# Gate and up of a channel mixer by seven products of quarters, with the matmuls pinned in the program's order

## The chip, the cores and the metric

The kernel runs on one core of one Trainium2 chip. The metric is the device time of one execution in microseconds (us). PE is the matrix engine (TensorE), PEld its weight loads, DVE VectorE, ACT ScalarE, POOL GpSimd, SP the engine that issues the DMAs of the weights.

## What is computed

A trunk of two layers on x of 256 tokens by 1024, all in float32. Each layer has a channel mixer, an attention part and a second channel mixer:

```python
for l in range(DEPTH):                      # 2
    x = x + 0.5 * swiglu(rms_norm(x, n1[l]), w_gate1[l], w_up1[l], w_down1[l])
    h = rms_norm(x, mix_norm[l])
    qa, ka, va, qb, kb, vb = split(h @ w_in[l])      # 1024 x 2304
    out_a = windowed_gqa_sink(qa, ka, va, sink[l])   # 8 heads, 2 key heads, ALiBi
    out_b = rms_norm(differential_attention(qb, kb, vb, lam)) * (1 - lam_init)   # 4 heads
    x = x + concat(out_a, out_b) @ w_out[l]          # 1024 x 1024
    x = x + 0.5 * swiglu(rms_norm(x, n2[l]), w_gate2[l], w_up2[l], w_down2[l])
return rms_norm(x, final_norm)
# swiglu(h, g, u, d) = (silu(h @ g) * (h @ u)) @ d, with g and u 1024 x 2816, d 2816 x 1024
```

The four mixers hold most of the arithmetic.

## The kernel before

**Products.** Every float32 factor is split in two parts of the type fp32r: `hi`, a rounded copy, and `lo`, what is left over. A product is three matmuls, hi times hi, lo times hi and hi times lo, added up in PSUM. For a product by tokens (`tokens`, lines 323 to 325) the activations are the stationary operand, 128 x 128, and 512 columns of weights stream past. `narrow` (lines 344 to 346) does it the other way round for the attention projections, with 256 tokens streaming.

**Weights.** A list `specs` holds all weight tiles in the order of use; most are 4 chunks of 128 rows by 512 columns (1 MB). `weights()` hands out the next tile and emits the loads up to two places ahead (`LOOK`). `emit_load` issues the DMA into `raw` (line 93), then for each half of the tile a cast on ACT (`whi`, line 109) and a subtraction on DVE (`wlo`, line 110). There are three buffers each of raw, whi and wlo. A scheduler orders each engine's instructions ahead of time by a simulated timeline; work inside `urgent()` has priority.

**A mixer** (`ffn`) works on the 2816 hidden columns in five groups of 512 and one of 256 (`NGRP` = 5). Group g computes gate and up (two tiles each, rows 0 to 511 and 512 to 1023, for both halves of the tokens: 96 matmuls), then the hidden by Silu on ACT (`gate`, line 395) and a scalar_tensor_tensor on DVE (`up`, line 401). Its down projection (two tiles, 48 matmuls) is done after the gate and up of group g + 1, from the hidden turned by transposes on PE (`turn`, line 415) and split in hi and lo (`split`, lines 329 and 330). Group 0 has no down of its own; its first two tiles, gate and up, are used in turns. After the last whole group come the quarter groups' gate and up in one tile, the down of group 4 for the left half of the output, the down of the remainder (`end`), and the down of group 4 for the right half. The down products stay in four of the eight PSUM banks throughout.

**Between stages.** `ffn_close` adds each finished half to the residual `xk` (line 375), transposes it (`Norm.pair`, line 182) and makes the next norm's operands: a scaled copy on ACT (line 190) and the left-over on DVE (line 191). The right half is turned inside the next stage (`late`).

**Attention** (`mix`) computes projections, scores, softmax, the two heads' outputs (`osl`, line 628; `oa`, line 670), the norm of the differential heads (`norm_b`, Squares at line 645), transposes them (`turned`, line 635) and multiplies by w_out.

Of the kernel before, what the change touches and what calls it, by code (L numbers as in the profile page):

```python
# [14 lines left out]
P = 128  # L15
# [7 lines left out]
HB = 4  # L23
# [4 lines left out]
LOOK = 2  # L28
N_RAW, N_HI, N_LO = 3, 3, 3
N_S4 = 18  # L30
# [3 lines left out]
def trunk(ctx: ExitStack, tc: tile.TileContext, x, n1, g1, u1, d1, nm, w_in, sink,  # L34
# [29 lines left out]

    def urgent():

        return tc.high_priority(300)


    specs = []  # L70
    loaded = {}
# [7 lines left out]
    def plain(w, c0, n, k0=0, kn=None):  # L79
        src = rows(w, c0, n, k0, kn)  # L80
        kn = src.shape[1]
        return (kn, n, lambda t: [(t, src)])

    def emit_load(i):
        kn, n, moves = specs[i]
        raw = wp.tile([P, kn, n], F32, tag="raw", bufs=N_RAW, name=nm_("raw"))
# [4 lines left out]
        for dst, src in moves(raw):  # L91
            if i > 1:
                sp.dma_start(dst, src)
            else:
                for a, b in zip(cuts, cuts[1:]):
                    sp.dma_start(dst[:, a:b], src[:, a:b])
                    yield
# [15 lines left out]
    nxt = [0, 0]  # L113

    def weights():
        i = nxt[0]
        nxt[0] += 1
        while i > 1 and nxt[1] <= min(i + LOOK, len(specs) - 1):
            for _ in emit_load(nxt[1]):
                pass  # L120
            nxt[1] += 1
        return loaded.pop(i)

    for l in range(DEPTH):
        def ffn_specs(wg, wu, wd):
# [3 lines left out]
            for g in range(1, NGRP):  # L129
                specs.extend(plain(w[l], g * 512, 512, k0, 4) for w in (wg, wu) for k0 in (0, 4))  # L130
                specs.extend(down(g - 1, h) for h in range(2))
            for k0 in (0, 4):
                def gu_moves(t, k0=k0, ws=(wg[l], wu[l])):
                    return [(t[:, :, h * 256:h * 256 + 256], rows(w, FF - 256, 256, k0, 4)) for h, w in enumerate(ws)]
                specs.append((4, 512, gu_moves))
# [10 lines left out]
        for c in range(2):  # L146
# [3 lines left out]
            specs.append((KC, 256, qa_moves))  # L150
# [5 lines left out]
        for k0 in (0, 2):  # L156
# [3 lines left out]
            specs.append((2, D, o_moves))  # L160
# [6 lines left out]
    class Norm:  # L167


        def __init__(self, g0):  # L170
            self.g0, self.xs = g0, []
            self.ss = tmp("nss", 2, (P, 2, 4))

        def squares(self, t, c, n):
            j_ = tmp("junk", 2, (P, 512))
            act.activation(j_[:, :n], xk[:, t, c:c + n], AF.Square, accum_out=self.ss[:, t, c // 256:c // 256 + 1])

        def pair(self, j):
            sl = halves(bank())
            for i in range(2):  # L180
                for t in range(2):
                    pe.transpose(sl[:, i, t * P:(t + 1) * P], xk[:, t, (2 * j + i) * P:(2 * j + i + 1) * P], ident)  # L182
            with urgent():
                self.operands(j, sl)

        def operands(self, j, sl):
            xs = blk()
            for i in range(2):
# [4 lines left out]
            self.xs.append(xs)  # L193
# [11 lines left out]
        def spread(self, sl):  # L205
# [4 lines left out]
            pe.matmul(sl[:, 0:S], lhsT=ones, rhs=dg, start=True, stop=True)  # L210
# [8 lines left out]
    early = [emit_load(0), emit_load(1)]  # L219
# [4 lines left out]
    nxt[1] = 2  # L224
# [27 lines left out]
    dist_i = const.tile([P, 512], mybir.dt.int32, name="dist_i")  # L252
# [7 lines left out]
    lin = const.tile([P, 4, DEPTH * 64], F32, name="lin")  # L260
    lsum = const.tile([P, 2, DEPTH], F32, name="lsum")
    lpr = const.tile([P, 2, DEPTH * 64], F32, name="lpr")
# [6 lines left out]
    def attention_constants():  # L269
# [6 lines left out]

        pool.iota(dist_i, pattern=[[P, 2], [-1, S]], base=0, channel_multiplier=1)
# [21 lines left out]

        for i, a in enumerate((lq1, lk1, lq2, lk2)):  # L300
            pool.dma_start(lin[:, i], a.rearrange("l d -> (l d)").partition_broadcast(P))

    def make_lam():
        for i in range(2):
# [11 lines left out]
    def tokens(accs, xs, w, k0, ks=range(4), first=0, last=KC - 1, tc=None):  # L316

        hi, lo = w
        for k, t in (tc or [(k, t) for k in ks for t in range(2)]):
# [3 lines left out]
            pe.matmul(accs[t], lhsT=xh, rhs=hi[:, k], start=kk == first, stop=False)  # L323
            pe.matmul(accs[t], lhsT=xl, rhs=hi[:, k], start=False, stop=False)  # L324
            pe.matmul(accs[t], lhsT=xh, rhs=lo[:, k], start=False, stop=kk == (last if isinstance(last, int) else last[t]))  # L325
# [11 lines left out]
    def narrow(acc, w, j, xs, kcs, first, last):  # L337

        hi, lo = w
        for i, (wk, xk) in enumerate(kcs):  # L340
# [3 lines left out]
            pe.matmul(acc, lhsT=wh, rhs=xv[:, 0:S], start=first and i == 0 and j == 0, stop=False)  # L344
            pe.matmul(acc, lhsT=wh, rhs=xv[:, S:512], start=False, stop=False)  # L345
            pe.matmul(acc, lhsT=wl, rhs=xv[:, 0:S], start=False, stop=last and i == len(kcs) - 1 and j == 1)  # L346
# [43 lines left out]
    def ffn(norm, aside=None, before=None, final=False):  # L390
# [11 lines left out]

        def hidden(gs, us):
# [5 lines left out]
        def turn(hs, n):  # L409
            out_ = []  # L410
            for i in range(n):
                sl = halves(bank())
                for c in range(2):
                    for t in range(2):
                        pe.transpose(sl[:, c, t * P:(t + 1) * P], hs[:, t, (2 * i + c) * P:(2 * i + c + 1) * P], ident)  # L415
# [8 lines left out]
        def down(hT, g, h, w):  # L424
            tokens(accs[h], [None] * (2 * g) + hT, w, 4 * g, last=(FC - 1, 4 * (NGRP - 1) - 1) if final and h else FC - 1)
# [42 lines left out]

        def end(h, tc=None, acc=None, c=0):
# [333 lines left out]
```

## Time and profile before

| what | us |
|---|---|
| median of three runs | 977.82 (977.58 to 980.34) |
| profiled execution | 978.65 |
| its span, from the first to the last instruction | 976.8 |
| PE busy | 954.5 |
| DVE busy | 549.9 |
| ACT busy | 475.7 |
| mean granted clock of PE | 0.996 |

Busy time says how long an engine had an instruction under way; matmuls overlap, so their own durations (390 ns) add up to more than PE's busy time, and the distance between their starts is what counts. A group line gives the busy time, the mean duration of one, then the idle time ahead of such instructions with what ended it.

### The profile page before, as it was taken

To read this page: it belongs to the slowest core of one execution; us is meant where nothing else is said; L and a number is where in the kernel's file an instruction comes from. 1 tells how busy PE (TensorE), PEld (TensorE's weight loads), DVE (VectorE), ACT (ScalarE), POOL (GpSimd) and SP (SyncE) were. 2 spreads that over 40 slices of the span, in tenths; PEclk is the share of its full clock that TensorE was granted. 3 is DMA by queue.
4 is the path that set the end of the run, shared out by engine and by line. 5 is a ranking of instruction groups with operands and counts; after the bars stand their busy time and mean duration, and the time that the engine had idled before them with its cause. 6 is when DMAs were issued, how large, how long until landed. Compare 5 with 4: busy or idle time off the path is not lost.

```text
span 976.8 us, 12379 instructions
## 1 busy us (share of the span) xinstructions
PE 954.5 (98%) x4940; PEld 809.3 (83%) x4940; DVE 549.9 (56%) x844; ACT 475.7 (49%) x809; POOL 21.2 (2%) x50
## 2 busy tenths in 40 slices
PE   7999999999999999999999999999999999999996
PEld 5888888889888888888878888887998888888885
DVE  5745445569846454555555454556696465545453
ACT  5644444457835543443544434436577464434442
POOL 3000000000000000000000000000000000000001
PEclk9999999999999999999999999999999999999999
DMA  9765555544524665555545656656444256565541
GB/s 269 260 206 182 174 193 193 176 135 166 131 85 143 211 206 175 194 191 179 193 144 181 201 181 188 197 174 196 148 140 122 87 172 205 182 211 198 173 129 43
DMA packets 98217, 169.38 MB, mean 173 GB/s; under 512 B 3182, under 2 KB 30896, under 8 KB 98160
## 3 DMA queue, kind: packets, MB, share of 16 engines
q1 hardware_dynamic: 96784, 167.26, 53.3%
q0 software_dynamic: 288, 0.30, 0.4%
q10 hardware_dynamic: 1088, 1.05, 0.3%
q8 instruction: 38, 0.62, 0.3%
q14 instruction: 19, 0.16, 0.1%
HBM read 167.54 MB, written 1.05 MB: 173 GB/s over the span
## 4 chain that ended last, share of the span: by engine, by line
PE 95%; DMA 2%; ACT 2%; issue 0%; DVE 0%; SPq 0%; POOLq 0%; POOL 0%; ACTq 0%
PE ps L323 26%; PE ps L324 26%; PE ps L325 26%; PE ps L344 3%; PE ps L345 3%; PE ps L346 3%; PE ps L415 2%; DMA raw<-in_ffn_w_gate_dram 2%; PE ps L670 1%; PE ps L523 1%; ACT whi L109 1%; PE ps L609 1%; PE ps L610 1%; PE ps L611 1%; PE ps L628 1%; PE ps L182 1%
## 5 line engine op out<-in xcount | busy, mean ns | idle before, releaser
L110 DVE TENSOR_TENSOR wlo<-raw,whi 128x1024 fp32r<-128x1024 f32 (+2 forms) x392 | 379.5, 1013 | 319.7 <-ACT whi L109 317.8
L109 ACT CAST whi<-raw 128x1024 fp32r<-128x1024 f32 (+2 forms) x392 | 323.3, 882 | 360.4 <-PE ps L324 327.7
L324 PE MATMUL ps<-whi,s 128*128 128x512 f32 x1126 | 438.3, 389 | 0.0
L323 PE MATMUL ps<-whi,s 128*128 128x512 f32 x1126 | 433.5, 392 | 3.1 <-ACT s L190 2.0
L325 PE MATMUL ps<-wlo,s 128*128 128x512 f32 x1126 | 436.4, 389 | 0.0
L323 PEld LDWEIGHTS ps<-whi,s 128*128 128x128 f32 x1126 | 211.3, 188 | 46.6 <-ACT s L190 2.2
L324 PEld LDWEIGHTS ps<-whi,s 128*128 128x128 f32 x1126 | 212.0, 188 | 43.4 <-DVE ms L197 0.4
L325 PEld LDWEIGHTS ps<-wlo,s 128*128 128x128 f32 x1126 | 211.8, 188 | 43.5
L344 PE MATMUL ps<-s,whi 128*128 128x256 f32 x224 | 63.3, 287 | 4.3 <-ACT s L190 4.3
L345 PE MATMUL ps<-s,whi 128*128 128x256 f32 x224 | 63.6, 285 | 0.0
L346 PE MATMUL ps<-s,wlo 128*128 128x256 f32 x224 | 63.1, 283 | 0.0
L395 ACT ACTIVATE tmp<-ps,r 128x512 f32<-128x512 f32 (+1 forms) x48 | 31.3, 651 | 61.3 <-PE ps L325 61.3
L401 DVE SCALAR_TENSOR_TENSOR s<-ps,hr,tmp 128x512 f32<-128x512 f32 (+1 forms) x48 | 32.6, 705 | 35.6 <-PE ps L325 26.0
L344 PEld LDWEIGHTS ps<-s,whi 128*128 128x128 f32 x224 | 42.4, 191 | 5.3 <-ACT s L190 4.8
L345 PEld LDWEIGHTS ps<-s,whi 128*128 128x128 f32 x224 | 42.9, 192 | 0.2
L346 PEld LDWEIGHTS ps<-s,wlo 128*128 128x128 f32 x224 | 42.9, 192 | 0.2
L330 DVE TENSOR_TENSOR s<-ps,s 128x512 fp32r<-128x512 f32 x48 | 30.9, 682 | 8.2 <-ACT s L329 8.2
L533 ACT ACTIVATE s<-s,negm 128x256 f32<-128x256 f32 x64 | 31.8, 499 | 7.6 <-DVE negm L531 7.6
L329 ACT CAST s<-ps 128x512 fp32r<-128x512 f32 x48 | 25.7, 583 | 12.0 <-PE ps L415 9.7
L190 ACT ACTIVATE s<-ps,gcol 128x256 fp32r<-128x256 f32 x48 | 20.7, 472 | 7.4 <-PE ps L182 4.1
L415 PE MATMUL ps<-ident,s 128*128 128x128 f32 x176 | 23.8, 272 | 0.0
L415 PEld LDWEIGHTS ps<-ident,s 128*128 128x128 f32 x176 | 20.7, 140 | 3.2
(114 smaller groups left out, 414.5 us busy)
## 6 DMA issues: line engine op xcount, KB each, us to landing
raw<-in_ffn_w_down_dram SPq DMA_DIRECT2D x44, 1024.0 KB, 5.0
raw<-in_ffn_w_gate_dram SPq DMA_DIRECT2D x39, 1024.0 KB, 5.2
raw<-in_ffn_w_up_dram SPq DMA_DIRECT2D x39, 1024.0 KB, 5.1
raw<-in_w_in_dram SPq DMA_DIRECT2D x14, 1024.0 KB, 5.3
raw<-in_ffn_w_gate_dram SPq DMA_DIRECT2D x8, 512.0 KB, 4.0
raw<-in_ffn_w_up_dram SPq DMA_DIRECT2D x8, 512.0 KB, 5.0
raw<-in_w_in_dram SPq DMA_DIRECT2D x8, 512.0 KB, 4.6
raw<-in_w_out_dram SPq DMA_DIRECT2D x4, 1024.0 KB, 4.9
```

Of the source, the lines that this page charges most:

```text
L109: act.copy(h_, r_)
L110: dve.tensor_tensor(l_, r_, f(h_), op=ALU.subtract)
L323: pe.matmul(accs[t], lhsT=xh, rhs=hi[:, k], start=kk == first, stop=False)
L324: pe.matmul(accs[t], lhsT=xl, rhs=hi[:, k], start=False, stop=False)
L325: pe.matmul(accs[t], lhsT=xh, rhs=lo[:, k], start=False, stop=kk == (last if isinstance(last, int) else last[t]))
L344: pe.matmul(acc, lhsT=wh, rhs=xv[:, 0:S], start=first and i == 0 and j == 0, stop=False)
L345: pe.matmul(acc, lhsT=wh, rhs=xv[:, S:512], start=False, stop=False)
L346: pe.matmul(acc, lhsT=wl, rhs=xv[:, 0:S], start=False, stop=last and i == len(kcs) - 1 and j == 1)
L395: act.activation(g[:, :n], acc, AF.Silu, scale=norm.r[:, t:t + 1])
L401: dve.scalar_tensor_tensor(h[:, t, :n], in0=acc, scalar=norm.hr[:, t:t + 1], in1=g, op0=ALU.mult, op1=ALU.mult)
L415: pe.transpose(sl[:, c, t * P:(t + 1) * P], hs[:, t, (2 * i + c) * P:(2 * i + c + 1) * P], ident)
L533: act.activation(e[:, t, c], e[:, t, c], AF.Exp, scale=-1.0, bias=negm[:, n:n + 1], accum_out=den[:, n:n + 1])
```

## The change

Three of the whole groups (1, 3 and 4) compute gate and up together by a scheme of seven products in place of eight (Strassen's, in Winograd's form). The activations are cut in quarters by tokens and by rows of the weights, the weights in four: a is the upper half of gate, b of up, c the lower half of up, d of gate. Four sums of activation quarters are made once per mixer (`make_sums`). The seven weight operands are, in order of use, a, b - a, c - b, c - b + a, d, d - c + b - a and c, made in place in the raw tiles by differences on DVE (`less`) before the usual cast and subtraction. Each product is 12 matmuls into one bank; `by_seven` adds them up on DVE with a copy of the first on ACT. A changed group has nine weight tiles to split in place of six, of which six are loaded.

The transposes of the hidden before come after the second product. All matmuls that go through `mm` and all transposes that go through `flip` are pinned behind the instruction of PE that is traced before them. DMA and splitting of a weight tile are emitted apart; raw has six buffers and the loads run up to eight places ahead. The end of a mixer is put in a new order (`ffn_end`), and so are Squares and one scaled copy in attention. The constants for attention are made ahead of group 3; some buffers are shared or fewer.

```diff
-LOOK = 2
-N_RAW, N_HI, N_LO = 3, 3, 3
-N_S4 = 18
+LOOK, AHEAD = 2, 8
+N_RAW, N_HI, N_LO = 6, 3, 3
+N_S4 = 16
+SEVEN = (1, 3, 4)
...
+    def mm(*a, **k):
+
+        tc.keep_in_program_order(pe.matmul(*a, **k))
+
+    def flip(*a):
+        tc.keep_in_program_order(pe.transpose(*a))
...
+    class Step:
+        def __init__(self, kn, n, moves, key=None, prep=None, src=None, free=None):
+            self.kn, self.n, self.moves, self.prep = kn, n, moves, prep
+            self.key = object() if key is None else key
+            self.src = self.key if src is None else src
+            self.free = [self.src] if free is None else free
...
+    def seven(wg, wu, c0, downs):
+
+        a, b, c, d = [object() for _ in range(4)]
+
+        def less(x, y, to):
+
+            def prep():
+                for h in (0, 2):
+                    x_, y_, t_ = [raws[i][:, h:h + 2] for i in (x, y, to)]
+                    dve.tensor_tensor(t_, x_, y_, op=ALU.subtract)
+            return prep
+
+        n = dict(kn=4, n=512, moves=None)
+        return [plain(wg, c0, 512, 0, 4, key=a, free=[]),
+                Step(4, 512, plain(wu, c0, 512, 0, 4).moves, key=b, prep=less(b, a, a), src=a, free=[]),
+                Step(4, 512, plain(wu, c0, 512, 4, 4).moves, key=c, prep=less(c, b, b), src=b),
+                Step(**n, prep=less(c, a, a), src=a, free=[]),
+                downs[0],
+                plain(wg, c0, 512, 4, 4, key=d, free=[]),
+                Step(**n, prep=less(d, a, d), src=d, free=[a, d]),
+                Step(**n, src=c),
+                downs[1]]
...
+    def emit_dma(i):
+        s = specs[i]
+        raws[s.key] = raw = wp.tile([P, s.kn, s.n], F32, tag="raw", bufs=N_RAW, name=nm_("raw"))
+        for dst, src in s.moves(raw):
+            if i > 1:
+                sp.dma_start(dst, src)
+            else:
+                for k in range(s.kn):
+                    sp.dma_start(dst[:, k:k + 1], src[:, k:k + 1])
+                    yield
+
+    def emit_split(i):
+        s = specs[i]
+        kn, n, raw = s.kn, s.n, raws[s.src]
         hi = wp.tile([P, kn, n], F32R, tag="whi", bufs=N_HI, name=nm_("whi"))
         lo = wp.tile([P, kn, n], F32R, tag="wlo", bufs=N_LO, name=nm_("wlo"))
...
+    at = dict(use=0, dma=2, prep=2, split=2)
 
     def weights():
-        i = nxt[0]
-        nxt[0] += 1
-        while i > 1 and nxt[1] <= min(i + LOOK, len(specs) - 1):
-            for _ in emit_load(nxt[1]):
-                pass
-            nxt[1] += 1
+        i = at["use"]
+        at["use"] += 1
+        if i > 1:
+            while True:
+
+                if at["split"] <= min(i + LOOK, len(specs) - 1) and at["prep"] > at["split"]:
+                    for _ in emit_split(at["split"]):
+                        pass
+                    at["split"] += 1
+                elif at["prep"] <= min(i + LOOK + 1, len(specs) - 1) and at["dma"] > at["prep"] and \
+                        (specs[at["prep"]].prep is None or at["split"] >= at["prep"]):
+                    if specs[at["prep"]].prep is not None:
+                        specs[at["prep"]].prep()
+                    at["prep"] += 1
+                elif at["dma"] < min(i + AHEAD, len(specs)) and (specs[at["dma"]].moves is None or len(raws) < N_RAW):
+                    if specs[at["dma"]].moves is not None:
+                        for _ in emit_dma(at["dma"]):
+                            pass
+                    at["dma"] += 1
+                else:
+                    break
         return loaded.pop(i)
...
+            if self.sums:
+                if j % 2 == 0:
+                    self.xg.append(blk(F32).rearrange("p a (c s) -> p (a c) s", c=2))
+                for i in range(2):
+                    act.activation(self.xg[j // 2][:, j % 2 * 2 + i], sl[:, i], AF.Identity,
+                                   scale=gcol[:, self.g0 + 2 * j + i:self.g0 + 2 * j + i + 1])
+                if j == 3:
+                    self.make_sums()
...
+        def make_sums(self):
+
+            (t0, t1), (b0, b1) = [(t[:, :, 0:P], t[:, :, P:S]) for t in self.xg]
+            self.sm = []
+
+            def make(x, y, op):
+                v = tmp().rearrange("p a (c s) -> p (a c) s", c=2)
+                dve.tensor_tensor(v, x, y, op=op)
+                sm = blk().rearrange("p a (c s) -> p (a c) s", c=2)
+                act.copy(sm[:, :, 0:P], v)
+                dve.tensor_tensor(sm[:, :, P:S], v, f(sm[:, :, 0:P]), op=ALU.subtract)
+                self.sm.append(sm)
+                return v
+
+            s1 = make(t1, b1, ALU.add)
+            s2 = make(s1, t0, ALU.subtract)
+            make(t0, t1, ALU.subtract)
+            make(b0, s2, ALU.subtract)
+
+        def quarter(self, t, b):
+
+            def of(k):
+                xv = self.xs[2 * b + k // 2][:, k % 2]
+                return xv[:, t * P:(t + 1) * P], xv[:, S + t * P:S + (t + 1) * P]
+            return of
+
+        def summed(self, i):
+            return lambda k: (self.sm[i][:, k, 0:P], self.sm[i][:, k, P:S])
...
+        def prod(xo):
+            hi, lo = weights()
+            acc = bank()
+            for k in range(4):
+                xh, xl = xo(k)
+                mm(acc, lhsT=xh, rhs=hi[:, k], start=k == 0, stop=False)
+                mm(acc, lhsT=xl, rhs=hi[:, k], start=False, stop=False)
+                mm(acc, lhsT=xh, rhs=lo[:, k], start=False, stop=k == 3)
+            return acc
+
+        def by_seven(h, g):
+
+            flat = lambda: tmp().rearrange("p a n -> p (a n)")
+
+            def plus(o, x, y):
+                with urgent():
+                    dve.tensor_tensor(o, x, y, op=ALU.add)
+                return o
+
+            acc = prod(norm.quarter(0, 0))
+            m1 = flat()
+            with urgent():
+                act.copy(m1, acc)
+            m5 = prod(norm.summed(0))
+            hT = turn(h, 2)
+            m7 = prod(norm.summed(2))
+            m6 = prod(norm.summed(1))
+            u2 = plus(flat(), m1, m6)
+            u3 = plus(flat(), u2, m7)
+            u1 = plus(flat(), u3, m5)
+            plus(u2, u2, m5)
+            down(hT, g - 1, 0, weights())
+            acc = prod(norm.quarter(0, 1))
+            h = blk(F32)
+            g0 = plus(m1, m1, acc)
+            with urgent():
+                act.activation(g0, g0, AF.Silu, scale=norm.r[:, 0:1])
+            acc = prod(norm.quarter(1, 1))
+            g1 = plus(u3, u3, acc)
+            with urgent():
+                act.activation(g1, g1, AF.Silu, scale=norm.r[:, 1:2])
+            up(h, u1, g1, 1)
+            acc = prod(norm.summed(3))
+            plus(u2, u2, acc)
+            up(h, u2, g0, 0)
+            down(hT, g - 1, 1, weights())
+            return h
+
...
         for g in range(1, NGRP):
-            if g > 1:
-                hT = turn(h, 2)
+            if g == 3 and aside is not None:
+                with tc.issue_after(norm.last.ins):
+                    aside()
+            if g in SEVEN:
+                h = by_seven(h, g)
+                continue
             gs = [bank(), bank()]
             tokens(gs, norm.xs, weights(), 0)
-            if g == 1:
-                hT = turn(h, 2)
+            hT = turn(h, 2)
             tokens(gs, norm.xs, weights(), 4)
             us = [bank(), bank()]
             for k0 in (0, 4):
@@ -453,34 +615,48 @@
             h = hidden(gs, us)
             for hh in range(2):
                 down(hT, g - 1, hh, weights())
-            if g == 2 and aside is not None:
-                with tc.issue_after(norm.last.ins):
-                    aside()
-
+
+        gu = [bank(), bank()]
+        tokens(gu, norm.xs, weights(), 0)
         hT = turn(h, 2)
-        gu = [bank(), bank()]
-        for k0 in (0, 4):
-            tokens(gu, norm.xs, weights(), k0)
+        tokens(gu, norm.xs, weights(), 4)
         h = hidden([b[:, 0:256] for b in gu], [b[:, 256:512] for b in gu])
-        down(hT, NGRP - 1, 0, weights())
-        hE = [None] * (2 * NGRP) + turn(h, 1)
-        wE = [t.rearrange("p k (h n) -> p h k n", h=2) for t in weights()]
-
-        def end(h, tc=None, acc=None, c=0):
-            tokens(accs[h] if acc is None else [acc, acc], hE, [t[:, h, :, c:c + 512 if acc is None else c + 256] for t in wE],
-                   4 * NGRP, range(2), 0, FC - 1, tc)
-
-        return accs, hT, end, weights
+        return accs, hT, lambda: turn(h, 1)
+
+    BY_TOKENS = [(k, t) for t in range(2) for k in range(2)]
+    G4 = 4 * (NGRP - 1)
+
+    def ffn_end(parts, last):
+
+        accs, hT, rest = parts
+        hT = [None] * (2 * (NGRP - 1)) + hT
+        hE = []
+        w = {0: weights()}
+
+        def group(h, order, a=None, c=slice(None), first=0):
+            tokens(a or accs[h], hT, [t[:, :, c] for t in w[h]], G4, first=first, last=last[h], order=order)
+
+        def tail(h, order=BY_TOKENS, a=None, c=slice(None)):
+            tokens(a or accs[h], [None] * (2 * NGRP) + hE, [t[:, h, :, c] for t in w["rest"]], 4 * NGRP, last=last[h], order=order)
+
+        group(0, [(k, t) for k in range(3) for t in range(2)])
+        hE.extend(rest())
+        group(0, [(3, t) for t in range(2)])
+        w["rest"] = [t.rearrange("p k (h n) -> p h k n", h=2) for t in weights()]
+        w[1] = weights()
+        return group, tail
 
     def ffn_close(parts, nxt):
-        accs, hT, end, w = parts
-        res = Residual(nxt, accs)
-        end(0, [(k, t) for t in range(2) for k in range(2)])
+        group, tail = ffn_end(parts, (FC - 1, G4 + 3))
+        res = Residual(nxt, parts[0])
+        group(1, [(0, t) for t in range(2)])
+        tail(0)
         for t in range(2):
             res.add(0, t)
-        tokens(accs[1], [None] * (2 * (NGRP - 1)) + hT, w(), 4 * (NGRP - 1), first=0, last=FC - 1)
+        tail(1)
+        group(1, [(k, t) for k in (1, 2) for t in range(2)])
         res.turn(0)
-        end(1, [(k, t) for t in range(2) for k in range(2)])
+        group(1, [(3, t) for t in range(2)])
         for t in range(2):
             res.add(1, t)
 
...
-        for t in range(2):
-            act.activation(vB[:, t], vsl[t], AF.Copy, scale=norm.r[:, t:t + 1])
+        act.activation(vB[:, 0], vsl[0], AF.Copy, scale=norm.r[:, 0:1])
+        dve.tensor_scalar_mul(vB[:, 1], vsl[1], norm.r[:, 1:2])
...
         def norm_b():
 
             ss = tmp("ss", 1, (P, 2, HB))
-            for h in range(HB):
-                for t in range(2):
-                    j_ = tmp("junk", 2, (P, P))
-                    act.activation(j_, osl[t][:, h * P:(h + 1) * P], AF.Square, accum_out=ss[:, t, h:h + 1])
+            for t in range(2):
+                sq = tmp().rearrange("p a n -> p (a n)")
+                act.activation(sq, osl[t], AF.Square)
+                dve.tensor_reduce(ss[:, t], sq.rearrange("p (h d) -> p h d", h=HB), axis=mybir.AxisListType.X, op=ALU.add)
...
-                        pe.matmul(oa[t][:, c * P + a * 64:c * P + a * 64 + 64], lhsT=pT[c][:, kc, c0:c0 + P],
+                        mm(oa[t][:, c * P + a * 64:c * P + a * 64 + 64], lhsT=pT[c][:, kc, c0:c0 + P],
...
```

Elsewhere `pe.matmul` and `pe.transpose` become `mm` and `flip` in `tokens`, `narrow`, `spread`, `pair`, `turn` and `turned`; the scores, the transposed probabilities and the value products stay as they were. Norms ahead of attention make no sums. The last mixer's end uses `ffn_end` too.

More of the change, by code (lines that the diff above doesn't have):

```diff
@@ L313, in make_lam, with tokens @@
             dve.tensor_scalar_mul(gsub[:, l:l + 1], gcol[:, 48 + l:49 + l], 1.0 - lam_init[l])
-    def tokens(accs, xs, w, k0, ks=range(4), first=0, last=KC - 1, tc=None):
+    def tokens(accs, xs, w, k0, ks=range(4), first=0, last=KC - 1, order=None):
         hi, lo = w
-        for k, t in (tc or [(k, t) for k in ks for t in range(2)]):
+        for k, t in (order or [(k, t) for k in ks for t in range(2)]):
             kk = k0 + k
@@ L753, in finish @@
             sp.dma_start(out[0, t * P:(t + 1) * P, j * 512:(j + 1) * 512], ob[:, j])
[L755 to L756 removed]
+    accs = parts[0]
+    group, tail = ffn_end(parts, ((FC - 1), FC - 1))
+    dve.tensor_tensor(xk[:, 1, 512:D], xk[:, 1, 512:D], accs[1][1], op=ALU.add)
+    group(1, [(k, 0) for k in range(2)])
+    tail(0)
     for t in range(2):
         close(t, 0, 512, accs[0][t])
[L759 to L763 removed]
+    group(1, [(k, 0) for k in (2, 3)])
+    tail(1, [(k, 0) for k in range(2)])
     close(0, 512, 512, accs[1][0])
@@ L767, in trunk @@
         acc = bank()[:, 0:256]
-        cols = [t[:, :, c:c + 256] for t in w]
-        tokens([None, acc], hT, cols, 4 * (NGRP - 1), first=4 * (NGRP - 1), last=FC - 1, tc=[(k, 1) for k in range(4)])
-        end(1, [(k, 1) for k in range(2)], acc, c)
+        cols = slice(c, c + 256)
+        group(1, [(k, 1) for k in range(4)], [None, acc], cols, G4)
+        tail(1, [(k, 1) for k in range(2)], [None, acc], cols)
         close(1, 512 + c, 256, acc)
```

96 lines of the change are left out of this document (45 added, 51 removed).

## The prediction

> **What bounds the kernel now.** I read the busy times first, then the waits of the matrix engine (PE), then one steady group of a channel mixer in three views: the windows, the costliest groups of instructions, and VectorE's (DVE's) timeline.
>
> ```profile
> PE 954.5 (98%) x4940; PEld 809.3 (83%) x4940; DVE 549.9 (56%) x844; ACT 475.7 (49%) x809; POOL 21.2 (2%) x50
> ```
>
> PE is busy 98% of 976.8 us: products that go away can pay in full, if whoever feeds PE keeps up. The waits of PE over the whole run (what waited, for whom: us in total, times, longest):
>
> ```profile
> PE ps L344 <- ACT s L190: 4.3, 2, 2.1
> PE ps L323 <- ACT s L190: 2.0, 1, 2.0
> PE ps L323 <- ACT s L658: 0.9, 2, 0.5
> PE ps L628 <- ACT v L617: 0.6, 2, 0.3
> ```
>
> Besides 6.5 us at the start, all PE waits for lies at joints of stages: three of some 2 us where a mixer ends and the next norm's operands (L190) are late, four below 0.5 us in attention. A steady group, and the clock behind the third joint (us, busy us of PE, PEld, DVE, ACT, POOL, granted clock, DMA):
>
> ```profile
> 391.40:424.90 33.50, 33.50 (x154) 27.81 (x153) 16.79 (x16) 14.10 (x17) 0.00 (x0) 1.00 0.58 188
> 491.00:494.70 3.70, 3.70 (x15) 3.22 (x14) 3.05 (x8) 2.36 (x6) 0.69 (x1) 0.54 0.85 270
> ```
>
> One group of 512 columns takes 33.5 us, PE without a gap; DVE works for half of it. DVE's part, and the forms that the change multiplies:
>
> ```profile
> L110 DVE TENSOR_TENSOR wlo<-raw,whi 128x1024 fp32r<-128x1024 f32 x256 | 302.1, 1221 | 296.2 <-ACT whi L109 294.4
> L109 ACT CAST whi<-raw 128x1024 fp32r<-128x1024 f32 x256 | 256.0, 1050 | 307.9 <-PE ps L324 306.7 <-DMA raw<-in_ffn_w_gate_dram 1.0
> L375 DVE TENSOR_TENSOR xk<-xk,ps 128x512 f32<-128x512 f32 x20 | 13.1, 682 | 4.4 <-PE ps L325 4.4
> ```
> ```profile
> 394.51 1.28 DVE L330 TENSOR_TENSOR s<-ps,s 128x512 fp32r<-128x512 f32 x2
> 409.47 2.36 DVE L110 TENSOR_TENSOR wlo<-raw,whi 128x1024 fp32r<-128x1024 f32 x2 [2.96 <-ACT whi L109]
> 413.37 1.43 DVE L401 SCALAR_TENSOR_TENSOR s<-ps,hr,tmp 128x512 f32<-128x512 f32 x2 [1.54 <-PE ps L325]
> ```
>
> Two instructions back to back start 2.36 - 1.22 = 1.14 us apart at 1024 elements, 1.28 - 0.68 = 0.60 at 512, 1.43 - 0.75 = 0.68 for L401: a queue is summed by these. ACT's cast waits for PE (306.7 us): a weight tile is split when PE has left the tile three places earlier, and DVE's idle time hangs on that. DVE's slack is what the change spends.
>
> **Matmuls.** In the timeline a tile of 24 matmuls lasts 5.44 us, 0.2265 each. Seven products of 12 take 84 instead of 96: 2.72 us less, so a changed group needs 33.5 - 2.7 = 30.8 us of PE. There are 12 (3 in each of 4 mixers): 32.6 us if PE stays the bound.
>
> **DVE in a changed group.** Before: 6 tiles at 2.28 (two halves), two ups, two splits of the turned hidden: 13.7 + 1.4 + 1.2 = 16.3 (the window has 16.8). After: 9 tiles (7 weight operands, 2 of down) 20.5; four differences of weights, two instructions each, 9.1 (no such f32 result of 1024 elements is in the trace; L110 is the same operation on the same operands in size and place, so 1.14; below it nothing speaks, above it 1.22 if none overlap); 7 additions with PSUM or tmp at 0.60 (L375's form) 4.2; ups 1.4, splits 1.2. Sum 36.4, and about 0.7 because four or five of the additions read what the instruction before them wrote (L281 to L282 in the start: 0.72 apart instead of 0.60). So 37.1 of DVE against 30.8 of PE: DVE becomes the bound of these groups unless it enters them with work done. The page "VectorE: DVE Perf Modes" of the Trainium skill (The TRN2 errata) gives (N+151)/0.96 ns for an f32 tensor_tensor, 1.224 us at 1024; L110's 1.221 agrees for one. Charged in full to each of the 26 long instructions this makes the group 2.2 us dearer and would turn the sum below to about 992 (pair 70.9, group 1 34.5); the 1.14 between starts decides against it.
>
> ACT: 9 tiles at 2 x 0.95, a copy, two Silus, two casts: about 21 of 30.8, no bound.
>
> **The lead.** Three buffers of whi and wlo: when PE starts a group's first product, DVE can have done A and B, and the differences for B and for C (they write raw, of which there are now six): 4 x 2.28 = 9.1. At the end, the last tile's second half must be ready 2.7 us before PE ends, and behind it come 1.3 (an addition, an up). One group alone, with full lead: 37.1 - 9.1 - 1.3 + 2.7 = 29.4, under 30.8, so hidden.
> - Group 3 follows a plain group, in which DVE is idle for half: 30.8.
> - Group 4 follows group 3 at once: the two need 74.2 - 9.1 - 1.3 + 2.7 = 66.5, before 67.0: -0.5 for the pair.
> - Group 1 follows group 0, whose first two tiles are held together and released late, and whose ups (1.4) and second half of B (1.1) fall into it: 29.4 + 2.5 = 31.9, with a Silu ahead of B's cast 32.3: -1.2.
> Together -1.7 per mixer, -6.8. Bounds: no lead at all, 37.1 in each, +3.6 x 12 = +43; all hidden, -32.6. I take the queue's sum because each of its rows is measured; only the lead is argued.
>
> **Sums of the activations**: 8 DVE instructions at 0.60, 4 casts at 0.54, 8 activations at 0.38 (L190) per mixer norm, in group 0, where DVE idles 4.3 us in one piece ahead of the next tiles' casts. Hidden there; if ACT is late, up to 3 us each. I take +0.3 x 4 = +1.2.
>
> **Joints.** The three waits of 2.15, 2.15, 1.97 stand behind eight transposes (L182) that were queued after the last matmul (195.62 against 195.40). Pinned in program order, they get 6 matmuls (1.36 us) and the second pair's transposes behind them as cover, against some 2 us that ACT and DVE need for the operands: I keep 0.6 each, so -4.5. The half clock behind the third (0.54 for 3.7 us in the window) goes with it: -1.7. Bounds: 0, if a cast or subtraction stands ahead in the queues; -8.0. The ffn's turned remainder gets 12 matmuls, 2.7 us, over a split of about 1.5: nothing.
>
> **Attention.** norm_b's eight Squares and their reads become two activations and two reductions, shortening the chain by over 1 us; its transposes are now ahead of the last 8 products (L670), which cover them; one vB goes to DVE. Of 1.5 us of waits I take back 1.2. If the chain of some 4.5 us outlasts the 24 products ahead (5.3 us by the 0.11 between records of L670), it costs 1 us per layer.
>
> **Start.** Split into DMA and splits with six raw buffers, the loads stay in one queue in order. The pinned order takes the scheduler's freedom to put matmuls on whi ahead of those on wlo, and the extra activations stand among the first casts: +1.0 (0 to 2.5). Fewer or renamed buffers (s4 16, junk 1) wait for nothing that is alive by my count: 0.
>
> **Sum**: -6.8 + 1.2 - 6.2 - 1.2 + 1.0 = -12.0. The profiled execution took 978.65 (span 976.8), 0.83 over the median 977.82 of the runs shown; 966.6 of its own time, about 966 in the median.
>
> **Rivals.**
> - DVE is the bound with hardly any lead (slower). Each weight now needs difference, cast, difference in turn through two in-order queues, and the urgent additions go ahead of splits. If groups 1 and 4 run at DVE's 37.1 and group 3 alone is hidden: (3.6 + 3.6 - 2.7) x 4 = +18, with the rest (-5.2) 990.6; if none is hidden, 1016. It decides once a changed group costs over 34.2 us on the mean. For it: 37.1 against 30.8. Against: the idle 296 us of DVE. Chance 0.28.
> - PE stays the bound, all hidden: -32.6 - 5.2, 940. Needs DVE ahead by more than I count. 0.11.
> - The pins give nothing (a wait moves from one joint to another): -12.0 + 6.2, 972; with groups that give nothing either, 979. 0.14.
> - The clock. A wait of 1.97 us was followed by half clock for 3.4 us, at 1.7 us of loss; two of 2.15 were not. If DVE's lag gathers in one wait of 2 us in each changed group, up to 12 x 1.7 = 20 more: 986. "TensorE: Matmul & The Clock Gate" of the Trainium skill (What's actually happening) has the clock fall only after an idle window of about 3.4 us, free-running; by that none of these waits would cost clock, and the trace's 1.97 speaks against the full window as a bound. 0.04.
> - That the change doesn't do what it says: the pin binds to the engine's instruction before, so it holds; no chance of its own.
> My forecast 0.43.
>
> **Chances.** A measurement tells about 0.3% (2.9 us). Faster: the forecast nearly whole, PE-bound, a third of the pins: 0.58. Slower: DVE-bound, the clock, none of the rest: 0.30. Same: 0.12. The range 944 to 992 takes in the bounds of the lead down to the fully hidden and up to the milder form of DVE's; the forecast's own is 957 to 974.
>
> **What would show it.** Groups of 30.8 us (group 3), 32 to 33 (1) and about 36 (4), with PE waiting for wlo of L110's successor; DVE busy about 810 us; 144 matmuls of 512 columns fewer; the waits for L190 below 1 us each and clock 1.00 around the third joint. Group 3 over 33 would break the lead; group 4 at 31 the price of DVE.

## The result and the profile after

The changed kernel takes 1010.49 us (1008.42 to 1011.3, 4 runs) against 978.96 before: 1.031 times as long (95% interval 1.030 to 1.033). Faster was forecast, 966, and 1010 lies above the range.

The busy times on the page of the changed kernel:

```profile
PE 946.1 (94%) x4796; PEld 790.2 (78%) x4796; DVE 808.2 (80%) x1134; ACT 579.5 (57%) x913; POOL 25.9 (3%) x50
```

144 matmuls fewer, as planned, and DVE at the 808 us that were counted (810). But PE is busy for 94% of a span of 1009.5 us. The waits of PE over the run (what waited, for whom: us in total, times, longest):

```profile
PE ps L68 <- DVE wlo L155: 26.5, 12, 3.3
PE ps L71 <- DVE s L512: 12.5, 7, 8.2
PE ps L341 <- DMA grow<-in_ffn_norm_dram: 6.3, 1, 6.3
PE ps L68 <- DVE s L441: 2.9, 8, 0.4
PE ps L68 <- DVE s L272: 2.7, 5, 1.4
PE ps L68 <- ACT s L271: 1.7, 3, 0.7
```

L68 is now every pinned matmul, L71 every pinned transpose, L155 the subtraction that makes wlo, L512 the up. The old waits for the norm's operands (L190, now L271 and L272) have shrunk, those for DVE are new: twelve for wlo, up to 3.3 us in one piece, and one of 8.2 us in the first mixer's group 1. The windows of groups 1, 3 and 4 of the second mixer, and of one stretch at the end of a wait in group 4 (us, busy us of PE, PEld, DVE, ACT, POOL, granted clock, DMA):

```profile
338.40:376.00 37.60, 33.23 (x141) 26.54 (x140) 37.39 (x41) 21.56 (x25) 0.00 (x0) 0.95 0.57 195
409.60:441.00 31.40, 31.07 (x141) 25.51 (x140) 31.03 (x33) 20.31 (x23) 0.00 (x0) 1.00 0.58 201
441.00:481.10 40.10, 34.94 (x141) 27.21 (x140) 36.58 (x38) 21.31 (x24) 0.00 (x0) 0.91 0.53 182
457.40:464.20 6.80, 5.87 (x14) 4.61 (x15) 6.80 (x8) 1.99 (x2) 0.00 (x0) 0.50 0.61 211
```

Group 3 runs in 31.4 us, near what was forecast. Group 4 takes 40.1, longer than DVE's busy 36.6: something other than DVE's amount of work is lost there, and the clock reads 0.50 for 6.8 us. What DVE did just ahead of that stretch:

```profile
449.05 1.22 DVE L111 TENSOR_TENSOR raw<-raw,raw 128x1024 f32<-128x1024 f32 x1
450.19 1.28 DVE L441 TENSOR_TENSOR s<-ps,s 128x512 fp32r<-128x512 f32 x2
451.39 6.89 DVE L155 TENSOR_TENSOR wlo<-raw,whi 128x1024 fp32r<-128x1024 f32 x6
458.20 2.35 DVE L111 TENSOR_TENSOR raw<-raw,raw 128x1024 f32<-128x1024 f32 x2
```

and PE:

```profile
452.65 0.50 PE L68 MATMUL ps<-wlo,s 128*128 128x512 f32 x1 [0.93 <-DVE wlo L155]
458.33 0.80 PE L68 MATMUL ps<-wlo,s 128*128 128x512 f32 x1 [3.33 <-DVE wlo L155]
```

DVE has no gap. It makes six halves of wlo in a row, and PE starts again only when the sixth is there. The program, read with its tile names, says which: the first half of the fourth product's tile, then both halves of the down tile and both of the fifth product's, and only as the sixth the second half of the fourth product's tile, on which PE stands. Four subtractions of 1.14 us went in front of the needed one. The casts on ACT stand in the same order, so even the needed half's whi is there only at 454.2. The scheduler fixed this order ahead of time. The needed half has to go through a difference first (it is the one at 449.05), and the tiles in front of it need none; that they counted as ready sooner in the scheduler's simulated timeline is inferred, and run 3 bears it out.

Group 1 has a shorter form of the same fault, with a wait of 2.95 us. There the two halves of the down tile and the two splits of the turned hidden (L441) stand in front of the needed half, which is the first of the three subtractions from 353.09 on:

```profile
348.49 3.49 DVE L155 TENSOR_TENSOR wlo<-raw,whi 128x1024 fp32r<-128x1024 f32 x3
351.89 1.28 DVE L441 TENSOR_TENSOR s<-ps,s 128x512 fp32r<-128x512 f32 x2
353.09 3.48 DVE L155 TENSOR_TENSOR wlo<-raw,whi 128x1024 fp32r<-128x1024 f32 x3
```

In group 3 the splits stand in the order of use, and no wait is above 0.4 us. Nor is their order turned round in the first mixer's group 1, whose 8.2 us have another cause (run 6).

### The profile page after: what moved, and what is told of

It reads as the page before. It is cut to its first block, busy times and chain, and to the rows that moved or that the text cites. A ratio compares the mean times of both kernels' runs of the same rounds, so it can differ in the third digit from the quotient of the medians.

```text
span 1009.5 us, 12588 instructions
## 1 busy us (share of the span) xinstructions
PE 946.1 (94%) x4796; PEld 790.2 (78%) x4796; DVE 808.2 (80%) x1134; ACT 579.5 (57%) x913; POOL 25.9 (3%) x50
## 4 chain that ended last, share of the span: by engine, by line
PE 68%; DVE 22%; issue 4%; DMA 2%; ACT 2%; POOL 1%; ACTq 0%; POOLq 0%; SPq 0%; DVEq 0%
PE ps L68 60%; DVE wlo L155 11%; DVE raw L111 5%; PE ps L71 2%; PE ps L699 1%; DVE tmp L530 1%; DMA raw<-in_ffn_w_gate_dram 1%; PE ps L764 1%; DVE s L441 1%; DVE tmp L282 1%; DVE s L272 1%; ACT whi L154 1%; DVE s L285 1%; PE ps L785 1%; PE ps L787 1%
## 5 line engine op out<-in xcount | busy, mean ns | idle before, releaser
L68 PE MATMUL ps<-whi,s 128*128 128x512 f32 (+1 forms) x2156 | 679.8, 397 | 9.8 <-DVE s L441 2.9
L154 ACT CAST whi<-raw 128x1024 fp32r<-128x1024 f32 (+2 forms) x464 | 396.6, 909 | 300.2 <-PE ps L68 167.5
L155 DVE TENSOR_TENSOR wlo<-raw,whi 128x1024 fp32r<-128x1024 f32 (+2 forms) x464 | 463.7, 1043 | 126.1 <-ACT whi L154 125.3
L68 PEld LDWEIGHTS ps<-whi,s 128*128 128x128 f32 x2156 | 408.4, 192 | 100.5 <-ACT whi L154 6.6
L68 PE MATMUL ps<-wlo,s 128*128 128x512 f32 (+1 forms) x1078 | 427.4, 396 | 26.7 <-DVE wlo L155 26.5
L68 PEld LDWEIGHTS ps<-wlo,s 128*128 128x128 f32 x1078 | 206.4, 192 | 76.6 <-DVE wlo L155 33.9
L111 DVE TENSOR_TENSOR raw<-raw,raw 128x1024 f32<-128x1024 f32 x96 | 114.6, 1216 | 0.0
L68 PE MATMUL ps<-s,whi 128*128 128x256 f32 x448 | 82.7, 286 | 0.4 <-DVE s L272 0.4
L68 PEld LDWEIGHTS ps<-s,whi 128*128 128x128 f32 x448 | 70.1, 192 | 1.6 <-DVE s L272 0.8
L68 PE MATMUL ps<-s,wlo 128*128 128x256 f32 x224 | 63.3, 283 | 0.0
L530 DVE TENSOR_TENSOR tmp<-tmp,ps 128x512 f32<-128x512 f32 x84 | 56.0, 679 | 0.0
L68 PEld LDWEIGHTS ps<-s,wlo 128*128 128x128 f32 x224 | 43.0, 192 | 0.0
L71 PE MATMUL ps<-ident,s 128*128 128x128 f32 x208 | 29.2, 280 | 12.6 <-DVE s L512 12.5
L71 PEld LDWEIGHTS ps<-ident,s 128*128 128x128 f32 x208 | 24.8, 144 | 17.9 <-issue 13.2
L441 DVE TENSOR_TENSOR s<-ps,s 128x512 fp32r<-128x512 f32 x48 | 31.0, 682 | 7.3 <-ACT s L440 7.3
L272 DVE SCALAR_TENSOR_TENSOR s<-ps,gcol,s 128x256 fp32r<-128x256 f32 x48 | 22.9, 481 | 15.4 <-ACT s L271 15.2
L271 ACT ACTIVATE s<-ps,gcol 128x256 fp32r<-128x256 f32 x48 | 22.5, 472 | 13.9 <-PE ps L71 8.7
L506 ACT ACTIVATE tmp<-ps,r 128x512 f32<-128x512 f32 (+1 forms) x24 | 14.6, 614 | 23.0 <-PE ps L68 22.6
L512 DVE SCALAR_TENSOR_TENSOR s<-ps,hr,tmp 128x512 f32<-128x512 f32 (+1 forms) x24 | 15.2, 657 | 14.3 <-ACT tmp L506 8.2
L310 POOL TENSOR_TENSOR r<-ms,mhalf 128x2 f32<-128x2 f32 x6 | 8.6, 1435 | 626.6 <-DVE ms L308 626.6
```

The source lines that it names most:

```text
L68: tc.keep_in_program_order(pe.matmul(*a, **k))
L71: tc.keep_in_program_order(pe.transpose(*a))
L111: dve.tensor_tensor(t_, x_, y_, op=ALU.subtract)
L154: act.copy(h_, r_)
L155: dve.tensor_tensor(l_, r_, f(h_), op=ALU.subtract)
L271: self.last_act = act.activation(xs[:, i, 0:S], sl[:, i], AF.Identity, scale=g)
```

## The experiments

Two theories were set against each other. **Queue**: DVE's 37 us of work per group is the bound, in whatever order. **Order**: the work would fit, but the order of the splits makes PE wait some 3 us in one piece, and the clock falls behind it.

**1. No group by seven products.** `SEVEN = ()`, and `self.sums` always False.

> The changed kernel with no group by seven products and no sums of the activations: only the loads, the pinned order, the new ends of the mixers and the attention edits are left. If the loss of 31 us comes from those, it stays at 1000 or more. If it comes from the changed groups, this run lies a little under the kernel before, about 973: three joint waits of 2 us and the half clock behind the third gone (-8), 1 us per layer lost in attention, 1 us at the start.

974.37 us, 0.995 of before (0.993 to 0.997). The rest of the change is no loss; the 36 us between this and the changed kernel come from the changed groups and their sums.

**2. Splits in the order of use.** Each cast and each subtraction of a tile is queued behind the one of the tile before (an edge for the order alone):

```diff
-                act.copy(h_, r_)
-                dve.tensor_tensor(l_, r_, f(h_), op=ALU.subtract)
+                for n_, ins in enumerate((act.copy(h_, r_), dve.tensor_tensor(l_, r_, f(h_), op=ALU.subtract))):
+                    if n_ in behind:
+                        tc.add_manual_dep(ins.ins, behind[n_], ...)
+                    if i > 1:
+                        behind[n_] = ins.ins.name
```

> The changed kernel with the splits of the weight tiles (cast on ACT, subtraction on DVE) chained in the order in which PE uses the tiles. Theory order: in groups 1 and 4 the scheduler has put four subtractions of later tiles ahead of the second half of the fourth product's tile; PE waits 3.0 and 3.3 us in one piece, and half clock follows. Then these waits and their clock go: 7 waits of 3.2 us are 22 us, the clock behind them up to 15, part of it comes back as shorter waits because DVE has no less to do: 975 to 990, mean clock over 0.985. Theory queue: DVE's 37 us per group is the bound whatever the order: within 5 us of 1010.

981.34 us, 1.0025 of before (1.0015 to 1.0034), mean clock 0.992 instead of 0.977. 29 of the 44 us between forecast and result were the order, on DVE and ACT together and with the clock behind it, with not one instruction less on DVE. Of the four subtractions named for both groups, group 1 had only two in front, beside two splits of the hidden. Group 4's window now:

```profile
432.20:466.20 34.00, 32.23 (x141) 25.23 (x141) 34.00 (x36) 21.24 (x24) 0.00 (x0) 1.00 0.53 182
```

DVE works all 34.0 us: here it is the bound, as the theory of the queue has it, but at 34.0 and not at 40. PE's waits are in pieces below 1 us there and the clock stays at 1.00. Over the run, one long wait is left, the transposes' 9.1 us in the first mixer:

```profile
PE ps L68 <- DVE wlo L155: 8.4, 15, 0.9
PE ps L71 <- DVE s L516: 13.4, 7, 9.1
```

**3. Without the differences of weights.** The call of `prep()` is left out.

> The changed kernel without the differences of weights on DVE (the products take the plain quarters, so gate and up are not those of the reference); nine tiles are still split. DVE's part of a changed group falls from 36.4 to 27.3 us, under PE's 30.8. Theory queue: all groups run at PE's 30.8, about 945 to 955. Theory order: the later tiles are ahead only because the differences hold up the needed one, so the waits go as well and it gives the same; if neither is right (pins, sums), it stays over 990.

951.77 us. Groups 1, 3, 4 take 30.8, 31.4, 31.4 outside the first mixer (group 1 takes 35.1 in it): with 27 us of work DVE is no bound. It does not tell the theories apart, but gives what the differences cost against run 2: 30 us. It also bears out what turned the splits round: in this program, with nothing for a tile to go through first, the scheduler left the splits of every changed group in the order of use.

**4. Groups 2 and 4 instead of 1, 3 and 4.** `SEVEN = (2, 4)`.

> Groups 2 and 4 by seven products in place of 1, 3 and 4: each has a plain group before it, in which DVE can work ahead. With a lead both are hidden, 30.8 us each: 2.7 x 8 = 22 us under a kernel without changed groups, so about 952 with the sums' cost, and clock over 0.99. If there is no lead, each costs 37.1, and it is 1000. If the order of the splits is bad in every changed group, 8 waits of 3 us and the clock make it 985.

959.01 us, 0.979 of before (0.977 to 0.981); the forecast of this run was 952. Each changed group takes 31.45 outside the first mixer, without any edit of the order: behind a plain group DVE has its lead, nothing is late, and the scheduler does not turn the splits round. The 7 us missing: 0.65 more per group (5), and a first mixer in which the plain group 1 takes 37.6 (4). These are 9; in the other direction, group 0 behind attention took 25.3 us here and 27.3 in run 1's profile, twice.

**5. Filling the waits.** In the changed kernel, 14 matmuls without use, about 3.2 us, ahead of the fourth product:

```diff
             m7 = prod(norm.summed(2))
+            if g != 3:
+                fill = bank()
+                for n_ in range(14):
+                    mm(fill, lhsT=norm.xs[0][:, 0, 0:P], rhs=norm.xs[0][:, 0], start=n_ == 0, stop=n_ == 13)
             m6 = prod(norm.summed(1))
```

> The changed kernel with 14 matmuls (3.2 us) of no use into a spare bank, ahead of the fourth product in groups 1 and 4, where PE waits 3.0 and 3.3 us for wlo. Outside the first mixer 31 us lie at half clock behind these waits. Theory clock: the matmuls fill the wait and keep the clock up, so more work takes about 12 to 15 us less: 995 to 1000, mean clock over 0.985. Without an effect of the clock of its own: 1010, or more where they come in the way of DVE.

1005.92 us, where 995 to 1000 was expected: less time with more work, but by 4.6 us only. The windows of groups 1 and 4:

```profile
338.40:376.00 37.60, 36.17 (x163) 29.41 (x162) 37.60 (x42) 23.14 (x28) 0.00 (x0) 1.00 0.54 186
441.00:481.00 40.00, 37.50 (x160) 30.04 (x159) 36.37 (x38) 22.51 (x25) 0.00 (x0) 0.96 0.59 191
```

In group 1 the clock stays at 1.00; it takes 36.0 instead of 37.6 from its first matmul to the next group's. Group 4 takes 39.0 instead of 40.1, with a wait of 2.1 us left and 3.4 us of half clock instead of 6.8. So the clock has a price of its own, 1 to 1.6 us in a group; most of such a wait is time in which the needed half is not there. The changed kernel shows the same price without any edit: in its fourth mixer group 1 waits 2.95 us, like the second and third mixers' group 1, but its clock stays at 1.00, and it takes 36.0. There the matmuls gain nothing. In the first mixer, where the fourth product had no such wait, they lose: group 1 takes 45.0 instead of 41.8, which is 3.2 us of the gain paid back.

**6. Group 1 of the first mixer plain**, splits in the order of use.

> The splits in the order of use, as before, and group 1 of the first mixer plain. In that mixer group 1 took 41.8 us in order, against 34.8 in the others: the transposes of the hidden wait 9.1 us for ups that wait for the norm's factor behind DVE's sums, differences and splits, and 10 us of half clock lie there. If the differences and splits of group 1 hold the factor up, the group falls to about 34 and the time from 981 to 973. If the sums alone do it, it stays at the 37.6 us that a plain group 1 took with groups 2 and 4 changed: 977.

974.04 us; that group takes 36.0 instead of 41.8. The time is the one expected if differences and splits hold the factor up, but the group lies between the two expectations: they cost 5.8 us there, and with the sums alone it is still 2.5 over the 33.5 that it takes in run 1, without sums. In the changed kernel the transposes there waited 8.2 us for the ups, the ups for half the norm's factor (hr), the factor for GpSimd. VectorE and GpSimd, with ms, r and hr (L308, L310, L312) in a chain:

```profile
39.58 0.16 DVE L308 TENSOR_SCALAR ms<-ms 128x2 f32<-128x2 f32 x1
39.65 2.35 DVE L155 TENSOR_TENSOR wlo<-raw,whi 128x1024 fp32r<-128x1024 f32 x2
...
44.96 0.17 DVE L312 TENSOR_SCALAR hr<-r 128x2 f32<-128x2 f32 x1 [0.63 <-POOL r L310]
45.04 3.49 DVE L155 TENSOR_TENSOR wlo<-raw,whi 128x1024 fp32r<-128x1024 f32 x3
...
48.78 1.40 DVE L512 SCALAR_TENSOR_TENSOR s<-ps,hr,tmp 128x512 f32<-128x512 f32 x2
```
```profile
39.82 5.11 POOL L310 TENSOR_TENSOR r<-ms,mhalf 128x2 f32<-128x2 f32 x1 [6.63 <-DVE ms L308]
```

Three losses in a row: ms stands behind sums and differences, the pow of two elements takes 5.11 us on GpSimd (0.94 in run 1), and hr is followed by three subtractions ahead of the ups.

**7. Differences on GpSimd**, splits in the order of use: `pool.tensor_tensor` in `less`.

> Splits in the order of use, and the differences of weights on GpSimd, which is idle: a tensor_tensor of 512 took 1.29 us there, so 8 of 1024 are about 20 us in a group of 31. If the two engines work side by side, DVE's part is 27.3 and the time near the 952 of the kernel without differences, 952 to 962. Against it: the factor's pow of two elements took 5.11 us on GpSimd in the changed kernel while DVE worked without a gap, 0.94 without changed groups. If GpSimd stands still while DVE is busy, the differences come late: over 990.

1052.47 us. VectorE's and GpSimd's groups, and what ScalarE's casts waited for:

```profile
L155 DVE TENSOR_TENSOR wlo<-raw,whi 128x1024 fp32r<-128x1024 f32 x328 | 485.7, 1520 | 86.1 <-ACT whi L155 84.4
L534 DVE TENSOR_TENSOR tmp<-tmp,ps 128x512 f32<-128x512 f32 x84 | 56.1, 679 | 0.4
```
```profile
L112 POOL TENSOR_TENSOR raw<-raw,raw 128x1024 f32<-128x1024 f32 x96 | 275.4, 2891 | 365.3 <-DVE wlo L155 271.3 <-issue 77.7 <-DMA raw<-in_ffn_w_up_dram 12.2
```
```profile
ACT whi L155 <- POOL raw L112: 168.1, 61, 5.9
```

The differences come late: a cast waits for one 61 times, up to 5.9 us. And the two engines slow each other: the subtraction with two operands in SBUF goes from 1218 to 1520 ns on the mean, the addition with one operand in PSUM stays at 679. "GPSIMD Engine Reference" of the Trainium skill (Specifications) has, in its table of the engine, the SBUF interfaces shared with VectorE and contention with instructions that read two SBUF inputs; these two rows agree.

**8. Sums later**: groups 2 and 4, splits in the order of use, `make_sums()` traced at the start of group 1 instead of in `pair`.

> Groups 2 and 4 changed, splits in the order of use, and the sums of the activations traced after group 0 instead of ahead of it. With groups 2 and 4 the first mixer's group 1, a plain one, took 37.6 us against 33.5 elsewhere. If the sums hold up the norm's factor, it falls to about 33.7 and the half clock there goes: 959 to 953 or 955. If not, 959.

957.41 us. The first mixer's group 1 falls to 34.4, where 33.7 was expected, and no half clock is left before the end; the time falls by 1.6, not by 4 to 6. The 37.6 of run 4 came from its profiled execution, the longest of its four (960.62, the others 958.7 to 959.3) and the only one with a mean clock of 0.996 instead of 0.999: by these clocks, the half clock in that group was in the expectation and not in the median.

**9. Both activations of a pair first.**

```diff
             for i in range(2):
                 g = ...
                 self.last_act = act.activation(xs[:, i, 0:S], sl[:, i], AF.Identity, scale=g)
+            for i in range(2):
+                g = ...
                 self.last = dve.scalar_tensor_tensor(xs[:, i, S:512], ...)
```

> The best kernel so far (groups 2 and 4, order of use, late sums), and in the norm's operands both activations of a pair issued before both DVE instructions. Behind attention PE waits 1.8 us in three pieces: the second activation of a pair is queued behind the first one's DVE instruction and a weight tile's 2 us of casts. If that is the cause, both joints lose their waits: 957.4 to about 953.5. If the casts alone stand ahead, 957.

951.83 us, 0.972 of before (0.971 to 0.974). Of the three waits at each joint behind attention two are gone; the first, of 0.45 us (L276), remains, and so does one of 0.3 us in each changed group for the split of the turned hidden (L445):

```profile
PE ps L68 <- DVE s L445: 2.7, 8, 0.3
PE ps L68 <- DVE s L276: 1.3, 3, 0.4
```

This version beats both kernels: two groups by seven products in each mixer, each behind a plain one.

**10. Group 3 alone.**

> The changed kernel with group 3 alone by seven products, and the scheduler's own order of the splits. In the changed kernel group 3 took 31.5 us, 2.1 under a plain one, with no split out of order. Four such groups on the kernel without changed groups (974.4) give 966, and 4 to 6 us more if the sums hold up the first mixer's group 1 (37.6 against 33.5): 970 to 972.

967.04 us, 0.988 of before (0.986 to 0.990), a little under what was expected: group 3 takes 31.45 in every mixer but the first (31.6), the first mixer's plain group 1 took 36.0, not 37.6.

## Why the prediction was wrong

From the first matmul of a group to that of the next, us:

| kernel | group 1, first mixer | group 1, others | group 3 | group 4 |
|---|---|---|---|---|
| before | 34.3 | 34.3 | 33.5 | 33.5 |
| forecast | 32.3 | 32.3 | 30.8 | 35.7 |
| changed | 41.8 | 36.0 to 37.6 | 31.5 | 39.3 to 40.1 |
| order of use (2) | 41.8 | 34.8 | 31.5 | 34.0 to 34.6 |

- **DVE's sum per group** was right: 37.1 forecast, 36.6 busy in group 4, 34.0 without a gap once the order was mended (part of the group's work is done ahead of it).
- **The lead** was right for group 3 and for the changed groups of run 4: hidden behind a plain group. For the pair 3 and 4 it gave 66.5; in the order of use it is 65.5. For group 1 it gave 32.3, and 34.8 was measured in the order of use, with waits of 1.4 us for the ups and 1.0 us for wlo in the second mixer. That group 0 leaves less lead than 9.1 minus 2.5 is the likely reason; no run shows it by itself.
- **The step that failed** is the one under "DVE in a changed group" and "The lead": the queue was summed as if its entries stood in the order in which PE needs them. Where the lead is used up, the scheduler's order decides, and it preferred what was ready to what was needed. It is worth 29 us, run 2 against the changed kernel, clock included. The rival that came nearest in time (DVE the bound with no lead, 1016) is not what happened: DVE's amount would have allowed 981 and, without the first mixer's loss, 974.
- **The clock** had 0.04 as a rival, with waits of 2 us in each changed group. It came: 44 us of the run lie at half clock, at most 22 us of loss, in spells behind the waits. Its own price is 1.6 us in group 1, where the clock was kept (run 5, and the fourth mixer of the changed kernel).
- **Sums and start**: "hidden there" was wrong for the first mixer, where the norm's factor came late. A plain group 1 takes 36.0 us there with the sums (runs 6 and 10) and 33.5 without (run 1), so the sums cost 2.5 us, where 2.2 had been allowed for sums and start together. The differences and splits of group 1 held the factor up further, at 5.8 us in that group and 7.3 in the time (run 6); the prediction has no such delay.
- **Joints**: the three waits of 2 us went, with the half clock of the third, as forecast. **Attention**: 1.2 was to be gained; instead each joint behind attention got waits of 0.45, 0.73 and 0.60 us, of which run 9 traces the last two to the operands' order on ACT. Run 1 has both in it: 974.4 where the forecast's terms give 971.4.

So of the 44 us, 29 are the order (run 2) and 7 the first mixer's group 1 (run 6). With run 6 at 974, 8 us remain to the 966 forecast, and the groups make them up: 3.7 in the first mixer's plain group 1, 2.5 in each of three groups 1, 0.7 in each of four groups 3, less 1.7 in each of three groups 4 and 1.1 in the first mixer's. Joints, attention, sums outside the first mixer's group 1, and start then came out near their sum, though not each near its term. Of the 0.65 in group 3, 0.3 is the wait for L441 that the page shows (2.9 us in 8 pieces, two in each mixer).

## What to carry to other kernels

When a change moves a second engine from half busy to nearly full, sum its queue by stage, and then read the order of its entries at the point where the lead runs out: an entry that needs one step more than its neighbours may have been put behind them. Chaining the entries in the order of use took no instruction more and was worth 29 us here; placing two loaded stages behind light ones instead of three gave 959 us against 981, and needed no edit of the order. A short chain of small instructions suffered most from the full queue here: the norm's factor waited in it at ms and again behind hr.

## What the runs showed of the hardware

- **Half clock follows from how a wait lies in time, not from its length alone.** In every trace with more than one, the spells of half clock begin on one grid of 3.413 us: those of the changed kernel at 355.02, 457.42 and 651.98 us stand 91, 121 and 178 steps behind the one at 44.41. In this kernel they last one, two or three steps (3.4, 6.8, 10.2 us). The same wait of 2.95 us in group 1 lies nearly whole in one step in the second mixer, and half clock follows; in the fourth mixer it is divided between two steps, and none follows:

```profile
351.60:355.00 3.40, 0.64 (x3) 0.55 (x4) 3.40 (x5) 0.00 (x0) 0.00 (x0) 1.00 0.56 151
355.00:358.40 3.40, 3.40 (x10) 2.62 (x9) 3.40 (x5) 0.58 (x1) 0.00 (x0) 0.50 0.43 163
843.10:846.50 3.40, 1.85 (x8) 1.05 (x6) 3.40 (x5) 1.99 (x3) 0.00 (x0) 1.00 0.49 191
846.50:849.90 3.40, 2.00 (x9) 1.65 (x10) 3.40 (x4) 0.00 (x0) 0.00 (x0) 1.00 0.94 307
```

  It also settles the prediction's 1.97 against two of 2.15: the 1.97 lies in one step, the others are divided into 0.8 and 1.4, and 1.0 and 1.1. Several short waits in one step do as well: in run 1, waits of 0.74 and 0.99 us (and the two like them in its fourth mixer) were enough:

```profile
298.00:304.10 6.10, 3.93 (x15) 2.41 (x14) 5.48 (x11) 3.95 (x8) 0.42 (x1) 1.00 0.65 188
304.10:307.50 3.40, 3.40 (x10) 2.66 (x9) 0.17 (x1) 0.00 (x0) 0.28 (x1) 0.51 0.75 284
```

  Over all the traces, without 12 us at each end, no step at full clock with PE idle for up to 1.58 us was followed by half clock, and every one with 1.93 us or more was; between 1.65 and 1.82 both came. "TensorE: Matmul & The Clock Gate" of the Trainium skill (What's actually happening) has a free-running window of 3413 ns; the spells' lengths agree with that, and so do their starts. Its rule that a whole idle window is needed does not agree with these waits; here the measurement decides.
- **GpSimd and VectorE slow each other** when VectorE reads two operands from SBUF: run 7's subtractions on VectorE went from 1218 to 1520 ns on the mean. On the other side, the factor's two elements took GpSimd 5.11 instead of 0.94 us in the changed kernel, while VectorE was busy with such subtractions for most of the time; that this is the cause is likely, not shown.
